# Last rows' weights ahead of the turning copies, a second turning tile, and two interleaved projections in a two-layer decoder trunk

## The chip, the cores and the metric

The kernel runs on one core of a Trainium2 chip. The metric is the time of one execution on the device, in microseconds, as the median of several runs. A profile of one execution goes with it. In profile rows PE is TensorE's matmuls, PEld its weight loads, DVE VectorE, ACT ScalarE, POOL GpSimd, SP SyncE; SPq and ACTq are DMA issues on SyncE's and ScalarE's queues.

## The reference

Two layers of a decoder for 256 tokens of width 2048, all in float32. Each layer is a mixer and a gated MLP, each with an RMS norm ahead and a residual sum behind:

```python
def reference(x, ...):
    for l in range(DEPTH):                  # 2
        h = rms_norm(x, mix_norm[l])
        h = mixer_ab(h, ...) if l % 2 == 0 else mixer_c(h, ...)
        x = x + h
        h = rms_norm(x, ffn_norm[l])
        x = x + conv_ffn(h, ffn_w_up[l], ffn_conv_w[l], ffn_conv_b[l], ffn_w_down[l])

def mixer_c(h, w_in, b_f, q_gain, k_gain, w_out):   # layer 1: attention with a forget gate
    q, k, v, g, f = jnp.split(h @ w_in, [D, 2*D, 3*D, 4*D], axis=-1)   # 16 heads of 128
    q, k = rms_norm(q, q_gain), rms_norm(k, k_gain)
    c = cumsum(log_sigmoid(f + b_f))                # one number a head and token
    s = q k^T * scale + c_query - c_key             # causal softmax in blocks of 128 queries
    return (softmax(s) @ v * sigmoid(g)) @ w_out

def conv_ffn(h, w_up, conv_w, conv_b, w_down):
    z = h @ w_up                                    # 2 x 5632 columns
    z = causal convolution of width 3 over tokens + conv_b
    a, b = jnp.split(z, 2, axis=-1)
    return (jax.nn.silu(a) * b) @ w_down
```

Mixer A/B of layer 0 (spatial gating and a gated linear recurrence) is not touched by the change.

## The kernel before

The residual stream x lies on chip as 16 blocks of 128 features by 256 tokens, in seven tiles (blocks 12 to 15 are one, x_76 in the program; blocks 8 to 11 are x_75). A norm (`Norm`) turns block m into a pair of tiles for TensorE, a high part rounded for the fast matmul and the rest: `feed_split`, L398 on ScalarE and L401 on VectorE. Weights are treated alike: each load of 512 KB on SyncE's queue (L198) gives a tile w, ScalarE copies its rounded part into wh (L185), VectorE subtracts the rest into wl (L186). Each product then takes three matmuls: high by high, high by rest, rest by high. Rings of five tiles for w and three for wh and wl, with some more in a second pool, let the loads run ahead.

A projection goes through k, the feature blocks, in pairs, one weight load a pair, and has the tokens' two halves T in two PSUM tiles. `project_tok` (L323) does it for four heads of q, k or v (L341 to L343 are its matmuls, 12 a pair), `project_four` (L346) for the MLPs and the output projections (L360 to L362), and `project` (L301) for one output block of 128 features with the features on partitions (L316).

A result with tokens on partitions has to be turned before it goes into x or into the heads. `blocks` turns 32 by 32 blocks on VectorE into a tile tmp (L373), and `moves` sends 16 small copies (L380) that put the blocks in their places, in turn on SyncE's queue and GpSimd's, for one quarter of the last MLP also on ScalarE's. `transposed` does both.

What runs beside the projections is written as generators: each call of `tick`, one ahead of every weight load, moves the waiting ones on by a step, so that their instructions land between the splits of the weights. `held` binds an instruction's place behind the last wh or wl before it. The framework's scheduler then sets each engine's order by its own estimates; no engine's queue is reordered on the chip.

Attention (`mixer_c`, from L941) begins with the first four heads' q and k, called `early` (L963 to L965): first all eight pairs of q, then all eight of k; `fetch` loads the forget gate's weights w_cf between. After them `drain` finishes the norm. `turn_rows` (L1137) then scales each of the two (L1140), squares and sums them for their norm (L433, L434, L1148) and turns them into `turn` tiles, which `attend` (L1041) takes. `forget` and `sums` (L976, L988) make c, a scan on VectorE (L1020), and send it through memory into cb (L1022, L1028).

In the MLP (`ffn`, L1254) `four` and `up` do the up-projection with the convolution, `down` the down-projection in four quarters q of four output blocks, summed over several groups of hidden features in y. In the last group `add_y` turns a quarter of y and adds it to x (L1335). In the last MLP the fourth quarter is done as four rows, blocks 12 to 15, by `project` (L1364); their result needs no turning and is added at L1368, and `finish_x` writes x out (L1351, L1353). There `room` gives one tile tmp and two tiles zt for the turning.

Of the kernel before, what the change touches and what calls it, by code (L numbers as in the profile page):

```python
# [55 lines left out]
def tile_trunk(ctx: ExitStack, tc: tile.TileContext, x, pp_d, cst_d, mlev_d, msk_d,  # L56
# [263 lines left out]
            done += c  # L320
        return ps

    def project_tok(wsrc, norm, room=None):  # L323

        ps = [pm.tile([P, 512], F32, tag="pm", name=nm("pm")) for _ in range(2)]
        for k in range(0, KT, 2):
            tick()
            wh, wl = weights(wsrc[:, k * 512:(k + 2) * 512], 1024, None, apart)
            if room is not None:
                ar = room()  # L330
                for i in range(2):
                    nc.gpsimd.tensor_copy(ar[:, i * S:(i + 1) * S].rearrange("p (u n) -> p u n", u=2),
                                          view(norm.a[k + i], S - 1, (S, 2), (-1, P)))
            for T in range(2):
                for i in range(2):
                    a = norm.a[k + i]
                    ah, al = a[:, T * P:(T + 1) * P], a[:, S + T * P:S + (T + 1) * P]
                    if T and room is not None:
                        ah, al = ar[:, i * S:i * S + P], ar[:, i * S + P:(i + 1) * S]
                    h, l = (by_two(t, i) for t in (wh, wl))  # L340
                    PE.matmul(to_two(ps[T]), ah, h, start=k + i == 0, stop=False)  # L341
                    PE.matmul(to_two(ps[T]), ah, l, start=False, stop=False)  # L342
                    deep["last"] = PE.matmul(to_two(ps[T]), al, h, start=False, stop=k + i == KT - 1)  # L343
# [597 lines left out]
    def mixer_c(norm):  # L941
# [18 lines left out]
            held(V.tensor_tensor(w2, w.rearrange("p (k c) -> p k c", k=KT)[..., 0:CH],  # L960
                                 pp[:, norm.col:norm.col + KT].unsqueeze(2).to_broadcast([P, KT, CH]), ALU.mult), "wl")

        early = [project_tok(w_cqkv[0], norm)]  # L963
        flight.append(fetch())
        early.append(project_tok(w_cqkv[CH // 4], norm))  # L965
        drain()
        depth[0] = 2
        Rt = norm.Rt
# [285 lines left out]
    def ffn(l, norm, last):  # L1254
# [5 lines left out]
        nxt = None if last else Norm(C_MIX + KT)  # L1260

        def room():
            return (hp.tile([P, 1024], F32, tag="tmp", name=nm("tmp"), bufs=1),
                    hp.tile([P, 4, S], F32, tag="zt", name=nm("zt"), bufs=2))

        def four(j0):
# [54 lines left out]

        y = hp.tile([P, 2, D], F32, tag="y", name=nm("y"))

        def add_y(q, finish):
            tmp, zt = room()
            near = last and q == 2
            transposed(lambda T: y[:, T, q * 512:(q + 1) * 512], tmp, zt,
                       (nc.sync, nc.gpsimd, SC) if near else (nc.sync, nc.gpsimd))

            def rest():  # L1330
                for _ in range(3 if near else LAG - 2 * (q == 3)):
                    yield
                for i in range(4):
                    m = 4 * q + i
                    held(V.tensor_tensor(xT[m], xT[m], zt[:, i], ALU.add), "wl")  # L1335
                    if finish:
                        finish_x(m)
                    if not near and (q < 3 or i % 2):
# [17 lines left out]

        def down(k0, hid, first, final):
            n = len(hid)
            for q in range(4):
                if last and final and q == 3:  # L1360
                    parts = None
                    for m in range(4 * q, KT):
                        end = m == KT - 1
                        ps = project(w_dn[l, m], hid, chunks=(n,), k0=k0, parts=parts)  # L1364
                        if not end:
                            tick()
                            parts = weights(w_dn[l, m + 1][:, k0 * P:(k0 + n) * P], n * P)
                        V.tensor_tensor(xT[m], xT[m], ps[:, 0:S], ALU.add)  # L1368
                        finish_x(m)
                    return  # L1370
                ps = project_four(w_dn[l, 4 * q:4 * q + 4], hid, n, k0)
                for T in range(2):
                    d = y[:, T, q * 512:(q + 1) * 512]
                    if first:
# [1 line left out]
                    else:  # L1376
                        V.tensor_tensor(cols4(d), cols4(d), of_rows(ps[T]), ALU.add)
                if final:
                    add_y(q, True)

        j0, k0, hid = 0, 0, []
        for g, (now, ahead) in enumerate(STEPS):
# [100 lines left out]
```

## Time and profile before

| | us |
|---|---|
| median of 3 runs (2170.22 to 2171.02) | 2170.75 |
| the profiled execution | 2170.68 |
| its span, first to last instruction | 2168.9 |
| TensorE busy with matmuls, 10874 of them | 2162.4 |
| VectorE busy | 1599.7 |
| ScalarE busy | 1310.1 |
| GpSimd busy | 470.7 |

The granted clock of TensorE is 1.0 over the span. HBM gives 202 GB/s on average. An instruction's row in order of time has its start, its duration, the engine and line, what it writes and reads, how many are merged, and, in brackets, how long its engine was idle before it and what released it.

### The profile page before, as it was taken

The page shows a single profiled execution, that of the slowest core. Times are in us where ns is not written, and L with a number is a line of the kernel's source. Part 1 is how long each engine was busy: PE and PEld are TensorE (multiplying, and loading weights), DVE is VectorE, ACT ScalarE, POOL GpSimd, SP SyncE. Part 2 cuts the span into 40 slices and gives each one's busy share as a digit, 9 for nine tenths or more (in the row PEclk, how much of TensorE's full clock was granted, in tenths as well). Part 3 has the DMA queues.
Part 4 walks back from the last instruction along what each step waited for, and adds up shares of the span by engine and source line. Part 5 has one row for each costly group of instructions (what it writes and reads, how often), then busy time and mean ns, then how long its engine had stood idle before and what let it go on. Part 6 is the DMA issues. An engine that isn't in the chain of part 4 may idle for free.

```text
span 2168.9 us, 32423 instructions
## 1 busy us (share of the span) xinstructions
PE 2162.4 (100%) x10874; PEld 1900.3 (88%) x10874; DVE 1599.7 (74%) x2265; ACT 1310.1 (60%) x1903; POOL 470.7 (22%) x867
## 2 busy tenths in 40 slices
PE   9999999999999999999999999999999999999999
PEld 8998888888888888888888888888888888888888
DVE  7888768777577657776887787877786577667766
ACT  6677766666466545654565556766666466456642
POOL 0352231212012002111133443221211012012102
PEclk9999999999999999999999999999999999999999
DMA  8755777777667767776777767777777677666866
GB/s 304 220 172 175 219 223 236 235 229 238 217 214 223 223 213 212 230 235 205 248 230 223 243 203 215 225 240 223 234 238 223 201 236 220 227 213 208 247 214 187
DMA packets 492680, 483.61 MB, mean 223 GB/s; under 512 B 115168, under 2 KB 460400, under 8 KB 492384
## 3 DMA queue, kind: packets, MB, share of 16 engines
q1 hardware_dynamic: 465888, 453.27, 66.4%
q0 software_dynamic: 24896, 26.05, 5.2%
q10 hardware_dynamic: 1728, 2.21, 0.4%
q8 instruction: 85, 1.39, 0.3%
q14 instruction: 83, 0.68, 0.1%
HBM read 435.24 MB, written 2.11 MB: 202 GB/s over the span
## 4 chain that ended last, share of the span: by engine, by line
PE 94%; DVE 2%; DMA 2%; SPq 1%; ACT 1%; issue 0%; DVEq 0%; ACTq 0%; POOLq 0%
PE pm L360 25%; PE pm L361 25%; PE pm L362 25%; PE pm L341 4%; PE pm L343 4%; PE pm L342 4%; PE pm L316 2%; PE pm L236 1%; DVE wl L186 1%; SPq L380 1%; DMA w<-in_w_up 1%; DMA zt<-tmp 1%; PE pm L260 0%; DVE tmp L373 0%; ACT wh L185 0%
## 5 line engine op out<-in xcount | busy, mean ns | idle before, releaser
L186 DVE TENSOR_TENSOR wl<-w,wh 128x1024 fp32r<-128x1024 f32 (+1 forms) x820 | 991.6, 1217 | 460.6 <-ACT wh L185 451.1
L185 ACT ACTIVATE wh<-w 128x1024 fp32r<-128x1024 f32 (+1 forms) x820 | 856.7, 1049 | 624.4 <-PE pm L362 459.3
L360 PE MATMUL pm<-wh,a 128*128 128x512 f32 x1728 | 655.8, 379 | 0.0
L361 PE MATMUL pm<-wl,a 128*128 128x512 f32 x1728 | 655.2, 379 | 0.2
L362 PE MATMUL pm<-wh,a 128*128 128x512 f32 x1728 | 654.9, 379 | 0.0
L380 POOL DMA_DIRECT2D zt<-tmp x413 | 223.5, 549 | 1134.8 <-DVE tmp L373 1022.9
L361 PEld LDWEIGHTS pm<-wl,a 128*128 128x128 f32 x1728 | 326.6, 189 | 47.1 <-DVE wl L186 1.0
L362 PEld LDWEIGHTS pm<-wh,a 128*128 128x128 f32 x1728 | 326.6, 189 | 46.3
L360 PEld LDWEIGHTS pm<-wh,a 128*128 128x128 f32 x1728 | 326.6, 189 | 46.3
L360 PE MATMUL pm<-wh,hid 128*128 128x512 f32 x688 | 260.8, 379 | 0.0
L361 PE MATMUL pm<-wl,hid 128*128 128x512 f32 x688 | 260.8, 379 | 0.0
L362 PE MATMUL pm<-wh,hid 128*128 128x512 f32 x688 | 260.8, 379 | 0.0
L341 PE MATMUL pm<-wh,a 128*128 128x512 f32 x416 | 158.7, 381 | 0.4 <-ACT a L398 0.4
L343 PE MATMUL pm<-wh,a 128*128 128x512 f32 x416 | 157.8, 379 | 0.0
L342 PE MATMUL pm<-wl,a 128*128 128x512 f32 x416 | 157.7, 379 | 0.0
L360 PEld LDWEIGHTS pm<-wh,hid 128*128 128x128 f32 x688 | 130.0, 189 | 18.5
L362 PEld LDWEIGHTS pm<-wh,hid 128*128 128x128 f32 x688 | 130.0, 189 | 18.4
L361 PEld LDWEIGHTS pm<-wl,hid 128*128 128x128 f32 x688 | 130.0, 189 | 18.4
L1289 ACT ACTIVATE conv<-zt,pp 128x256 f32<-128x256 f32 x176 | 95.8, 589 | 71.5 <-DMA zt<-tmp 48.4
L380 POOL DMA_DIRECT2D turn<-tmp x160 | 86.9, 551 | 211.4 <-DVE tmp L373 179.3
L1290 DVE SCALAR_TENSOR_TENSOR conv<-zt,pp,conv 128x255 f32<-128x255 f32 x176 | 80.2, 480 | 54.4 <-ACT conv L1289 42.7
L373 DVE STREAM_TRANSPOSE tmp<-z 128x512 f32<-128x512 f32 x120 | 98.1, 850 | 7.1 <-ACT z L1275 5.1
(255 smaller groups left out, 2207.7 us busy)
## 6 DMA issues: line engine op xcount, KB each, us to landing
w<-in_w_up SPq DMA_DIRECT2D x352, 512.0 KB, 5.0
w<-in_w_dn SPq DMA_DIRECT2D x176, 512.0 KB, 5.0
w<-in_w_cqkv SPq DMA_DIRECT2D x96, 512.0 KB, 4.9
w<-in_w_abo SPq DMA_DIRECT2D x32, 512.0 KB, 5.0
w<-in_w_cg SPq DMA_DIRECT2D x32, 512.0 KB, 5.2
w<-in_w_co SPq DMA_DIRECT2D x32, 512.0 KB, 4.8
zt<-tmp SPq DMA_DIRECT2D x414, 32.0 KB, 2.7
zt<-tmp POOLq DMA_DIRECT2D x413, 32.0 KB, 2.4
```

The lines of the kernel that those rows point to most:

```text
L185: r = deep["wh"] = SC.activation(wh, w, AF.Copy)
L186: deep["wl"] = V.tensor_tensor(wl, w, wh.bitcast(F32), ALU.subtract)
L341: PE.matmul(to_two(ps[T]), ah, h, start=k + i == 0, stop=False)
L342: PE.matmul(to_two(ps[T]), ah, l, start=False, stop=False)
L343: deep["last"] = PE.matmul(to_two(ps[T]), al, h, start=False, stop=k + i == KT - 1)
L360: PE.matmul(to_rows(ps[T]), ah, h, start=not begun and k + i == ks[0], stop=False)
L361: PE.matmul(to_rows(ps[T]), ah, l, start=False, stop=False)
L362: deep["mm"] = deep["last"] = PE.matmul(to_rows(ps[T]), al, h, start=False, stop=not more and k + i == ks[-1] + 1)
L373: V.transpose(tmp.rearrange("p (b m i t) -> p b m i t", b=4, m=4, t=2)[:, :, :, :, T], src(T).rearrange("p (m b j) -> p b m j", m=4, b=4))
L380: queues[(a + b) % len(queues)].dma_start(dst[BLK * b:BLK * (b + 1), :, a * n:(a + 1) * n], tmp[BLK * a:BLK * (a + 1), b * 4 * n:(b + 1) * ...
L1289: held(SC.activation(c, z, AF.Identity, bias=pp[:, cb:cb + 1], scale=w(2)))
L1290: V.scalar_tensor_tensor(c[:, 1:], z[:, :S - 1], w(1), c[:, 1:], ALU.mult, ALU.add)
```

## The change

It has three parts.

In the last MLP the weights of the last four rows are fetched and split in `split_rows`: two ahead of the sum of the third quarter into y, two more between that quarter's `blocks` and its `moves`, so all four ahead of the copies. Before, the first load stood at the row's `project` and each further one after the row ahead of it. `add_y` is split in two for it, the rows' loop has one `tick` more ahead, and the adds of the last two rows are bound behind the last add of the third quarter (`deep["near"]`).

In both MLPs `room` has two tiles tmp in place of one.

In the attention the q and k projections of the first four heads are cut in two: six pairs of q, six of k, then the last two pairs (blocks 12 to 15) of q, and of k.

```diff
--- before.py
+++ after.py
@@ -320,10 +320,10 @@
             done += c
         return ps
 
-    def project_tok(wsrc, norm, room=None):
-
-        ps = [pm.tile([P, 512], F32, tag="pm", name=nm("pm")) for _ in range(2)]
-        for k in range(0, KT, 2):
+    def project_tok(wsrc, norm, room=None, ks=range(0, KT, 2), ps=None):
+
+        ps = ps or [pm.tile([P, 512], F32, tag="pm", name=nm("pm")) for _ in range(2)]
+        for k in ks:
             tick()
             wh, wl = weights(wsrc[:, k * 512:(k + 2) * 512], 1024, None, apart)
             if room is not None:
@@ -960,9 +960,14 @@
             held(V.tensor_tensor(w2, w.rearrange("p (k c) -> p k c", k=KT)[..., 0:CH],
                                  pp[:, norm.col:norm.col + KT].unsqueeze(2).to_broadcast([P, KT, CH]), ALU.mult), "wl")
 
-        early = [project_tok(w_cqkv[0], norm)]
-        flight.append(fetch())
-        early.append(project_tok(w_cqkv[CH // 4], norm))
+        firsts = [w_cqkv[0], w_cqkv[CH // 4]]
+        early = []
+        for src in firsts:
+            early.append(project_tok(src, norm, ks=range(0, KT - 4, 2)))
+            if src is firsts[0]:
+                flight.append(fetch())
+        for src, ps in zip(firsts, early):
+            project_tok(src, norm, ks=range(KT - 4, KT, 2), ps=ps)
         drain()
         depth[0] = 2
         Rt = norm.Rt
@@ -1260,7 +1265,7 @@
         nxt = None if last else Norm(C_MIX + KT)
 
         def room():
-            return (hp.tile([P, 1024], F32, tag="tmp", name=nm("tmp"), bufs=1),
+            return (hp.tile([P, 1024], F32, tag="tmp", name=nm("tmp"), bufs=2),
                     hp.tile([P, 4, S], F32, tag="zt", name=nm("zt"), bufs=2))
 
         def four(j0):
@@ -1321,18 +1326,21 @@
 
         y = hp.tile([P, 2, D], F32, tag="y", name=nm("y"))
 
-        def add_y(q, finish):
+        def add_y(q, finish, between=None):
             tmp, zt = room()
             near = last and q == 2
-            transposed(lambda T: y[:, T, q * 512:(q + 1) * 512], tmp, zt,
-                       (nc.sync, nc.gpsimd, SC) if near else (nc.sync, nc.gpsimd))
+            blocks(lambda T: y[:, T, q * 512:(q + 1) * 512], tmp)
+            if between is not None:
+                between()
+            moves(tmp, zt, (nc.sync, nc.gpsimd, SC) if near else (nc.sync, nc.gpsimd))
 
             def rest():
                 for _ in range(3 if near else LAG - 2 * (q == 3)):
                     yield
                 for i in range(4):
                     m = 4 * q + i
-                    held(V.tensor_tensor(xT[m], xT[m], zt[:, i], ALU.add), "wl")
+                    deep["near"] = V.tensor_tensor(xT[m], xT[m], zt[:, i], ALU.add)
+                    held(deep["near"], "wl")
                     if finish:
                         finish_x(m)
                     if not near and (q < 3 or i % 2):
@@ -1356,19 +1364,26 @@
 
         def down(k0, hid, first, final):
             n = len(hid)
+            rows = []
+
+            def split_rows(count):
+                for m in range(KT - 4 + len(rows), KT - 4 + len(rows) + count):
+                    rows.append(weights(w_dn[l, m][:, k0 * P:(k0 + n) * P], n * P))
+
             for q in range(4):
                 if last and final and q == 3:
-                    parts = None
+                    tick()
                     for m in range(4 * q, KT):
-                        end = m == KT - 1
-                        ps = project(w_dn[l, m], hid, chunks=(n,), k0=k0, parts=parts)
-                        if not end:
+                        ps = project(w_dn[l, m], hid, chunks=(n,), k0=k0, parts=rows.pop(0))
+                        if m < KT - 1:
                             tick()
-                            parts = weights(w_dn[l, m + 1][:, k0 * P:(k0 + n) * P], n * P)
-                        V.tensor_tensor(xT[m], xT[m], ps[:, 0:S], ALU.add)
+                        r = V.tensor_tensor(xT[m], xT[m], ps[:, 0:S], ALU.add)
+                        if m >= KT - 2:
+                            tc.add_manual_dep(r.ins, deep["near"].ins.name, order, reason="not before")
                         finish_x(m)
                     return
                 ps = project_four(w_dn[l, 4 * q:4 * q + 4], hid, n, k0)
+                split_rows(2 if last and final and q == 2 else 0)
                 for T in range(2):
                     d = y[:, T, q * 512:(q + 1) * 512]
                     if first:
@@ -1376,7 +1391,7 @@
                     else:
                         V.tensor_tensor(cols4(d), cols4(d), of_rows(ps[T]), ALU.add)
                 if final:
-                    add_y(q, True)
+                    add_y(q, True, (lambda: split_rows(2)) if last and q == 2 else None)
 
         j0, k0, hid = 0, 0, []
         for g, (now, ahead) in enumerate(STEPS):
```

The matmuls and their number stay, and each engine's order changes in two places only, the beginning of the attention and the end of the program. SyncE at the beginning of the attention, before (w are weights; turn_10619 is q, turn_10624 is k, of the first four heads):

```order
L198 DMA w_10825<-in_w_cqkv 128x1024
L198 DMA w_10850<-in_w_cqkv 128x1024
L380 DMA turn_10619<-tmp_10621 32x4x64 x8
L198 DMA w_10876<-in_w_cqkv 128x1024
L198 DMA w_10908<-in_w_cqkv 128x1024
L380 DMA turn_10624<-tmp_10626 32x4x64 x8
L198 DMA w_10926<-in_w_cqkv 128x1024
```

and now:

```order
L198 DMA w_10825<-in_w_cqkv 128x1024
L198 DMA w_10850<-in_w_cqkv 128x1024
L198 DMA w_10876<-in_w_cqkv 128x1024
L380 DMA turn_10619<-tmp_10621 32x4x64 x8
L380 DMA turn_10624<-tmp_10626 32x4x64 x8
L198 DMA w_10908<-in_w_cqkv 128x1024
L198 DMA w_10926<-in_w_cqkv 128x1024
```

Both loads between the two groups of copies have left: one stands ahead of the first group, the other (w_10908, the first weights of the next heads' q) behind the second.

VectorE there, before, from the scaling of q (z_10620) to the turning of k (z_10625):

```order
L1148 TENSOR_TENSOR z_10620<-z_10620,ss_10618 128x512 x2
L186 TENSOR_TENSOR wl_10701<-w_10699,wh_10700 128x2x2x256
L373 STREAM_TRANSPOSE tmp_10621<-z_10620 128x512 x2
L186 TENSOR_TENSOR wl_10755<-w_10753,wh_10754 128x2x2x256
L433 TENSOR_TENSOR tmp_10626<-z_10625 128x512
L434 TENSOR_REDUCE ss_10618<-tmp_10626 128x4
L433 TENSOR_TENSOR tmp_10626<-z_10625 128x512
L434 TENSOR_REDUCE ss_10618<-tmp_10626 128x4
L186 TENSOR_TENSOR wl_10773<-w_10771,wh_10772 128x2x2x256
L425 TENSOR_SCALAR rm_10689<-ss_10618 128x2x4
L428 SCALAR_TENSOR_TENSOR rt_10690<-ss_10618 128x2x4
L429 TENSOR_TENSOR rt_10690<-rt_10690,rm_10689 128x2x4
```

and now:

```order
L434 TENSOR_REDUCE ss_10618<-tmp_10626 128x4
L1153 TENSOR_TENSOR z_10620<-z_10620,ss_10618 128x512 x2
L425 TENSOR_SCALAR rm_10689<-ss_10618 128x2x4
L373 STREAM_TRANSPOSE tmp_10621<-z_10620 128x512
L428 SCALAR_TENSOR_TENSOR rt_10690<-ss_10618 128x2x4
L373 STREAM_TRANSPOSE tmp_10621<-z_10620 128x512
L429 TENSOR_TENSOR rt_10690<-rt_10690,rm_10689 128x2x4
L186 TENSOR_TENSOR wl_10773<-w_10771,wh_10772 128x2x2x256
L430 SCALAR_TENSOR_TENSOR ss_10618<-rt_10690,ss_10618 128x2x4
L186 TENSOR_TENSOR wl_10791<-w_10789,wh_10790 128x2x2x256
L1153 TENSOR_TENSOR z_10625<-z_10625,ss_10618 128x512 x2
L373 STREAM_TRANSPOSE tmp_10626<-z_10625 128x512 x2
```

The turning of q has moved down behind the sums of squares of k, and two splits of weights stand ahead of the scaling of k where one stood.

A little before, ScalarE splits the last blocks of x for the norm. Before (a_10338 is block 10, a_10345 and a_10352 are blocks 12 and 13, a_10377 is block 11):

```order
L398 ACTIVATE a_10338<-x_75,pp 128x256
L455 ACTIVATE sq_10341<-x_75 128x256
L185 ACTIVATE wh_10416<-w_10415 128x2x2x256
L398 ACTIVATE a_10345<-x_76,pp 128x256
L455 ACTIVATE sq_10348<-x_76 128x256
L398 ACTIVATE a_10352<-x_76,pp 128x256
L455 ACTIVATE sq_10355<-x_76 128x256
L398 ACTIVATE a_10377<-x_75,pp 128x256
L455 ACTIVATE sq_10380<-x_75 128x256
```

and now:

```order
L398 ACTIVATE a_10338<-x_75,pp 128x256
L455 ACTIVATE sq_10341<-x_75 128x256
L185 ACTIVATE wh_10418<-w_10417 128x2x2x256
L398 ACTIVATE a_10345<-x_76,pp 128x256
L455 ACTIVATE sq_10348<-x_76 128x256
L398 ACTIVATE a_10352<-x_76,pp 128x256
L455 ACTIVATE sq_10355<-x_76 128x256
L398 ACTIVATE a_10377<-x_75,pp 128x256
L455 ACTIVATE sq_10380<-x_75 128x256
```

Nothing has moved there but the weight's number: block 11 stands behind blocks 12 and 13.

SyncE at the end, before (zt_20618 is the third quarter's turning, w_20745 the last row's weights, out<-x_76 the rows' results):

```order
L380 DMA zt_20518<-tmp_20517 32x4x64 x8
L1353 DMA out<-x_70 128x256
L1353 DMA out<-x_71 128x256
L1353 DMA out<-x_72 128x512
L198 DMA w_20745<-in_w_dn 128x1024
L380 DMA zt_20618<-tmp_20617 32x4x64 x6
L1351 DMA out<-x_76 128x256 x2
```

and now (zt_20630 and w_20639 are these):

```order
L380 DMA zt_20518<-tmp_20517 32x4x64 x8
L1361 DMA out<-x_70 128x256
L1361 DMA out<-x_71 128x256
L198 DMA w_20639<-in_w_dn 128x1024
L1359 DMA out<-x_76 128x256
L380 DMA zt_20630<-tmp_20629 32x4x64 x6
L1361 DMA out<-x_72 128x512
L1359 DMA out<-x_76 128x256
```

The last row's weights stand ahead of the write of x_72, and the first row's result is written ahead of the turning copies.

ScalarE at the end, before:

```order
L185 ACTIVATE wh_20640<-w_20639 128x1024
L185 ACTIVATE wh_20672<-w_20671 128x1024
L185 ACTIVATE wh_20706<-w_20705 128x1024
L380 DMA zt_20618<-tmp_20617 32x4x64 x5
L185 ACTIVATE wh_20746<-w_20745 128x1024
```

and now:

```order
L185 ACTIVATE wh_20616<-w_20615 128x1024
L185 ACTIVATE wh_20622<-w_20621 128x1024
L185 ACTIVATE wh_20634<-w_20633 128x1024
L185 ACTIVATE wh_20640<-w_20639 128x1024
L380 DMA zt_20630<-tmp_20629 32x4x64 x5
```

The split of the last row's weights has moved ahead of the five copies.

## The prediction

> **What bounds the kernel now.** I read the busy times first, then TensorE's waits, then the instructions by time at the two places that the change touches.
>
> ```profile
> span 2168.9 us, 32423 instructions
> PE 2162.4 (100%) x10874; PEld 1900.3 (88%) x10874; DVE 1599.7 (74%) x2265; ACT 1310.1 (60%) x1903; POOL 470.7 (22%) x867
> ```
>
> TensorE is busy for 2162.4 of 2168.9 us. The change leaves it the same matmuls, so nothing can be won beyond 6.5 us of idle time and the small gaps that the modelled ends hide. Of TensorE's waits the longest after the program's start is this one (total, times, longest):
>
> ```profile
> PE pm L341 <- ACT a L398: 0.4, 1, 0.4
> ```
>
> It lies in the attention layer's first projection; none lies in an MLP before the last rows. In order of time (start, duration, idle before), with the ScalarE split that releases it:
>
> ```profile
> 1057.06 0.49 ACT L398 ACTIVATE a<-x,pp 128x256 fp32r<-128x256 f32 x1
> 1057.60 0.48 PE L341 MATMUL pm<-wh,a 128*128 128x512 f32 x1 [0.42 <-ACT a L398]
> ```
>
> The rest of the idle time is the end. There, by engine (the four queues are TensorE, ScalarE's DMA issues and work, SyncE's issues, VectorE):
>
> ```profile
> 2161.48 0.61 PE L316 MATMUL pm<-hid,wh 128*128 128x256 f32 x4
> 2162.23 0.49 PE L316 MATMUL pm<-hid,wl 128*128 128x256 f32 x2
> 2163.90 0.61 PE L316 MATMUL pm<-hid,wh 128*128 128x256 f32 x4
> 2164.34 0.39 PE L316 MATMUL pm<-hid,wl 128*128 128x256 f32 x2
> ...
> 2155.56 4.17 ACTq L380 DMA_DIRECT2D zt<-tmp  x5
> 2159.86 1.06 ACT L185 ACTIVATE wh<-w 128x1024 fp32r<-128x1024 f32 x1 [10.34 <-DMA zt<-tmp]
> ...
> 2151.24 3.05 SPq L1353 DMA_DIRECT2D out<-x  x3
> 2154.34 0.42 SPq L198 DMA_DIRECT2D w<-in_w_dn  x1
> 2155.55 4.62 SPq L380 DMA_DIRECT2D zt<-tmp  x6
> 2164.64 1.21 SPq L1351 DMA_DIRECT2D out<-x  x2
> ...
> 2156.32 0.42 DVE L1368 TENSOR_TENSOR x<-x,pm 128x256 f32<-128x256 f32 x1 [0.53 <-PE pm L316]
> 2162.09 2.10 DVE L1335 TENSOR_TENSOR x<-x,zt 128x256 f32<-128x256 f32 x6
> 2164.77 0.42 DVE L1368 TENSOR_TENSOR x<-x,pm 128x256 f32<-128x256 f32 x1 [0.25 <-PE pm L316]
> ```
>
> The last row's weights are split only after ScalarE has issued five turning copies, so TensorE's wl matmuls begin 0.75 us after the wh matmuls ahead of them, where the last group needs 0.44 (2163.90 to 2164.34): 0.3 us lost, and 0.1 more in the longer wl matmuls (0.49 against 0.39). VectorE's last add ends at 2165.19, and SyncE's last write-out and its landing end the span at 2168.9.
>
> **The last rows' weights: +1.0 us.** The 0.4 us on TensorE goes away. What matters is what is late next. In the new order SyncE loads the last row's weights right after the two small writes (2152.33, where the third write of x stood, against 2154.34), and ScalarE splits them before its five copies instead of behind them. The landing times of the weight loads in this stretch (least, median, most):
>
> ```profile
> DMA to landing us min/median/max: 3.9/4.6/5.9
> ...
> zt<-tmp ACTq DMA_DIRECT2D x5, 32.0 KB, 3.1
> ```
>
> I take 3.9, since no other weight load stands behind this one: landed at 2156.2, split until 2157.3, so ScalarE's copies begin at 2157.4 instead of 2155.56, 1.8 us later. On SyncE the six copies now stand behind the write of row 12, which waits for its add (2156.32 + 0.42): 2156.8, then 0.5 for the issue, so 2157.3 instead of 2155.55. Both queues that carry the third quarter's turning are some 1.8 us late. In the old run ScalarE had issued its copies by 2155.56 + 4.17 = 2159.73, the last begun some 0.6 earlier, at 2159.1; now it begins at 2160.9 and lands 3.1 later (the second row above) at 2164.0. Four adds of 0.35 (2.10 / 6) bring 2165.4, and the new order keeps the adds of rows 14 and 15 behind them: 0.35 + 0.42, so 2166.2 against 2165.19. That is 1.0 us later, and the write-out follows as before. With 4.6 for the load it is 1.7, with 5.9 it is 3.0; if the copies catch up entirely, only the 0.4 us of TensorE is left as a gain. I keep +1.0, in -0.4 to +3.0.
>
> The Trainium skill (Trainium Kernel Development and Optimization, Key Constraints) says that issuing DMAs from several engines only saves the sequencers' issue time. By that rule the late start on ScalarE could be moved to any queue without loss, but the new order fills both queues at once; no run here separates the two.
>
> **The interleaved projections: +1.5 us.** First, what they do not remove. TensorE's stall at 1057.60 is for normed block 11 (sixth pair, second half). The new order still needs block 11 in its sixth pair, and ScalarE still splits 12 and 13 ahead of it. So the 0.4 us stays; only blocks 12 to 15 get more time, and nothing waits for them now. The load of w_cf goes ahead of one weight load; the splits there run some 5 us ahead of their use, which hides it.
>
> Second, what they delay. The first projection now ends two pairs (5.2 us) before the second instead of eight. Its squares, scaling and turning on VectorE fall together with those of the second, and its eight SyncE copies come directly before the second's eight, where a weight load or two stood between. The old run:
>
> ```profile
> 1085.33 5.12 SPq L380 DMA_DIRECT2D turn<-tmp  x8
> 1090.54 1.02 SPq L198 DMA_DIRECT2D w<-in_w_cqkv  x2
> 1094.33 5.10 SPq L380 DMA_DIRECT2D turn<-tmp  x8
> ...
> 1081.40 1.29 DVE L1148 TENSOR_TENSOR z<-z,ss 128x512 f32<-128x512 f32 x2
> 1086.29 0.67 DVE L433 TENSOR_TENSOR tmp<-z 128x512 f32<-128x512 f32 x1
> 1092.75 1.55 DVE L373 STREAM_TRANSPOSE tmp<-z 128x512 f32<-128x512 f32 x2
> 1103.41 1.19 DVE L186 TENSOR_TENSOR wl<-w,wh 128x1024 fp32r<-128x1024 f32 x1
> ...
> 1102.23 1.04 ACT L185 ACTIVATE wh<-w 128x1024 fp32r<-128x1024 f32 x1
> 1104.80 1.06 ACT L185 ACTIVATE wh<-w 128x1024 fp32r<-128x1024 f32 x1 [1.53 <-DMA w<-in_w_cqkv]
> 1105.77 0.45 ACT L1054 ACTIVATE k<-turn,gq 128x128 f32<-128x128 f32 x1
> 1108.03 1.04 ACT L185 ACTIVATE wh<-w 128x1024 fp32r<-128x1024 f32 x1
> 1109.10 0.69 ACT L1167 ACTIVATE vh<-pm,Rt 128x512 fp32r<-128x512 f32 x1
> ...
> 1109.47 0.38 PE L342 MATMUL pm<-wl,a 128*128 128x512 f32 x1
> 1114.65 0.38 PE L342 MATMUL pm<-wl,a 128*128 128x512 f32 x1
> ...
> DMA to landing us min/median/max: 3.6/4.8/6.3
> ```
>
> VectorE went from the second projection's first square (1086.29) to the end of its turning (1092.75 + 1.55 = 1094.3). Now the first projection's scaling (1.29) and turning (1.55), three small operations (0.6 together) and one more wl (1.2) lie between, and 0.7 of idle time and a small operation go: 1098.3. Only then does SyncE issue the second eight copies, 5.1 us, and behind them the weights of the next projection's first pair (the load that went out at 1090.54 + 0.6): 1103.5. They land 4.8 later (the median of this stretch; 3.6 and 6.3 are its ends) at 1108.3, wh takes 1.06, wl 1.2: 1110.6. TensorE read this wl at 1109.47, so it waits 1.15. Behind that, ScalarE's new order is wh, wh, the two copies of v (1.15 from 1109.10 on), the heads' splits (1105.77 to 1108.03, 2.3), and only then the third pair's wh: 1109.4 + 1.06 + 1.15 + 2.3 + 1.04 = 1114.9, its wl 1116.15, against 1114.65 + 1.15: another 0.35. Together 1.5; with 3.6 it is 0.3, with 6.3 it is 3.0.
>
> By the Trainium skill (DMA: Bandwidth & Descriptors, Anatomy of one DMA) a load takes about 2.0 us plus its bytes over 436 GB/s, an estimate of 3.2 us for 512 KB, with which this stall would be 0; the 4.8 us of the row speaks against it.
>
> **The second turning tile: 0.** Where VectorE waits at the turning line, it is
>
> ```profile
> DVE tmp L373 <- ACT z L1275: 5.1, 18, 0.8
> ```
>
> for ScalarE's z, and no row of VectorE's waits has it waiting there for the copies that read tmp. The order of all engines in the MLPs, up to the end, is unchanged, and TensorE waits for nothing there. Were the 5.1 us hidden waits for tmp after all, they would be 18 of 0.3 us, under TensorE's pairs of 2.6. I take 0, in -0.4 to 0.
>
> **Sum.** 1.0 + 1.5 + 0 = +2.5 us. The profiled execution took 2170.68 us, 1.8 more than its span, and the median is 2170.75: 2173.2 us.
>
> **Rivals.**
> Room enough (0.18): the loads land at their shortest, 3.6 and 3.9, and the turning copies overtake what they lost. Then 0.3 at the attention and 0 at the end: 2171.0. For it speaks that half the loads land below the median; against it, that the late copies at the end follow from an add and a split, not from a load.
> The stalls go (0.08): the 0.4 at the end, block 11's 0.4, as much again in the slowed matmuls behind it, and 0.4 hidden in the MLPs: 2170.75 - 1.6 = 2169.1. Against it: block 11's split keeps its place, and the end is set by adds.
> The forget gate becomes late (0.12), the case on the slower side of the bound below. Its scan stands behind the turning on VectorE, two copies through memory behind it, and the scores wait for these:
>
> ```profile
> 1102.81 0.68 DVE L1020 TENSOR_TENSOR_SCAN rows<-rows 16x256 f32<-16x256 f32 x1
> 1118.02 0.35 DVE L1073 SCALAR_TENSOR_TENSOR sc<-px,ct,cb 128x128 f32<-128x128 f32 x1 [1.07 <-PE px L1068]
> ...
> cb<-cd POOLq DMA_DIRECT2D x4, 512.0 KB, 4.2
> cd<-rows POOLq DMA_DIRECT2D x1, 16.0 KB, 4.9
> ```
>
> With the same delay of 4 us and its root moved behind the turning (0.9), the scan ends at 1108.4, and 4.9 + 4.2 later, 1117.5, the sums are there, 0.5 before their use. It decides from 0.5 us more. Three more put 2.5 us of waiting on VectorE at 1118 and, wl being queued behind it, on TensorE: 2173.2 + 2.5 = 2175.7. Against it: VectorE has idle time in that stretch that could take up the delay.
>
> **How the numbers follow.** The forecast has 0.62. Its own range runs from the smaller bounds (0.3 and 0.3: 2171.3) to one of the larger (3.0 + 1.0, or 1.5 + 3.0: 2175.2). With the rivals I reach from 2169.9 to 2176.0; outside lie most of the stalls' rival and the worst of the last. About 0.2% (4.3 us) is what a measurement can tell from no change, so 2166.4 and 2175.1 are the bounds: faster 0.01, since even all stalls together do not give it; slower 0.17 (the forget gate's case and 0.05 of the forecast); the same 0.82.
>
> **What would show it.** In the new profile TensorE should wait at L341/L342 near 1110 and 1116 us, for ACT or DVE, behind a weight load issued near 1103.5; the wait for block 11 near 1057.6 should still be there. At the end no idle time before the wl matmuls, the ScalarE copies starting after 2157, and VectorE's adds of rows 8 to 11 ending after row 15's matmuls. I am wrong if the next projection's first weights go out before 1102.3, or if the last add follows TensorE's end at once. TensorE's clock or matmul count changing would also break it.

## The result, and the profile after

The changed kernel takes 2174.49 us (median of 22 runs, 2173.57 to 2175.89), the kernel before in the same comparison 2170.8 (22 runs, 2169.28 to 2172.95): a ratio of 1.0018, with a 95% interval of 1.0012 to 1.0024, or 3.7 us more in median. The forecast was 2173.2 in 2169.9 to 2176.0, and "the same" within 0.2%. The time lies in the range. The interval does not contain 1, so the change does cost a little. The reason given for the time holds only in part.

The page of the changed kernel, and TensorE's waits over the whole span (total, times, longest):

```profile
span 2172.8 us, 32416 instructions
PE 2163.1 (100%) x10874; PEld 1902.9 (88%) x10874; DVE 1599.0 (74%) x2265; ACT 1310.0 (60%) x1903; POOL 470.5 (22%) x867
```

```profile
PE warm L143 <- DVE ones L85: 1.1, 1, 1.1
PE pm L342 <- DVE wl L186: 0.4, 2, 0.2
```

The span has grown by 3.9 us, TensorE's busy time by 0.7. The wait for block 11 (L341), before the longest behind the program's start, is gone, and two waits at L342, for the weights' rest, are new. They are the two that the prediction named. Small as they are, they can't make 3.9 us. The end can. The waits of the last 23 us:

```profile
POOL zt L380 <- DVE x L1342: 10.0, 1, 10.0
ACT wh L185 <- DMA w<-in_w_dn: 7.6, 1, 7.6
DVE x L1342 <- DMA out<-x: 4.3, 1, 4.3
```

and the same stretch in order of time, engine by engine (TensorE, VectorE, ScalarE, GpSimd, SyncE):

```profile
2164.51 0.39 PE L316 MATMUL pm<-hid,wl 128*128 128x256 f32 x2
...
2155.04 0.76 DVE L373 STREAM_TRANSPOSE tmp<-y 128x512 f32<-128x512 f32 x1
2156.89 0.42 DVE L1380 TENSOR_TENSOR x<-x,pm 128x256 f32<-128x256 f32 x1 [1.10 <-PE pm L316]
2158.73 1.23 DVE L186 TENSOR_TENSOR wl<-w,wh 128x1024 fp32r<-128x1024 f32 x1 [1.42 <-ACT wh L185]
2159.88 1.42 DVE L1342 TENSOR_TENSOR x<-x,zt 128x256 f32<-128x256 f32 x4
...
2166.63 1.43 DVE L1342 TENSOR_TENSOR x<-x,zt 128x256 f32<-128x256 f32 x4 [4.33 <-DMA out<-x]
2167.98 0.74 DVE L1380 TENSOR_TENSOR x<-x,pm 128x256 f32<-128x256 f32 x2
...
2157.64 1.06 ACT L185 ACTIVATE wh<-w 128x1024 fp32r<-128x1024 f32 x1 [7.55 <-DMA w<-in_w_dn]
2160.66 3.51 ACTq L380 DMA_DIRECT2D zt<-tmp  x5
...
2160.93 2.71 POOL L380 DMA_DIRECT2D zt<-tmp  x5 [10.02 <-DVE x L1342]
...
2152.92 1.26 SPq L198 DMA_DIRECT2D w<-in_w_dn  x1
2157.34 0.33 SPq L1359 DMA_DIRECT2D out<-x  x1
2160.66 3.82 SPq L380 DMA_DIRECT2D zt<-tmp  x6
```

Three queues start the third quarter's turning copies within 0.3 us of each other, at 2160.66, 2160.66 and 2160.93, although their own queues were free at different times: SyncE at 2157.34 + 0.33, ScalarE at 2157.64 + 1.06 = 2158.70 at the latest, and GpSimd had nothing to do for 10 us. What they read, tmp, was complete at 2155.04 + 0.76 = 2155.80. So they wait for something common that comes near 2160.6, and GpSimd's row names it: an add at L1342 on VectorE. In the group of four that starts at 2159.88 the first two adds end 0.76 later, at 2160.64. These are the adds of blocks 2 and 3, of the first quarter. They read the first quarter's zt tile. The MLP has two zt tiles, used in turn, so the third quarter's copies write into that very tile. The name in the row is a sign and not yet a proof: in the kernel before the same wait names an add as well,

```profile
POOL zt L380 <- DVE x L1335: 5.5, 1, 5.5
```

though there the copies on SyncE started at 2155.55 (in the prediction's rows), right behind the end of the turning at 2155.52, and no add of the shared tile was open. own_zt below is the test.

In the kernel before, the last of these adds stood ahead of two more splits of weights:

```profile
2147.65 0.43 DVE L1335 TENSOR_TENSOR x<-x,zt 128x256 f32<-128x256 f32 x1
```

It ended at 2148.08, 7.5 us before the copies wanted the tile. Now it ends at 2160.64, behind the last row's wl, since `held` keeps these adds in the written order of the splits and all four splits are written ahead of them. The last add of all ends at 2167.98 + 0.74 = 2168.72 instead of 2165.19; TensorE's last matmuls end at 2164.51 + 0.39 = 2164.90 instead of 2164.73. The 3.5 us between the two ends of the last add are nearly all of the loss. (The row of the 4.33 us names a write-out as the releaser. Those adds read zt; the last of SyncE's copies begins at 2163.9, and the last five copies of the three queues took 2.1 to 2.7 us from issue to landing, so I read the wait as the copies'. The profile of inter8 below, with the same end, names the copies for it: 4.27 us, zt<-tmp.)

The other place, the attention (SyncE, ScalarE, VectorE, TensorE of the changed kernel):

```profile
1091.41 11.43 SPq L380 DMA_DIRECT2D turn<-tmp  x16
1102.93 8.03 SPq L198 DMA_DIRECT2D w<-in_w_cqkv  x7
...
1107.06 1.06 ACT L185 ACTIVATE wh<-w 128x1024 fp32r<-128x1024 f32 x1 [2.54 <-DMA w<-in_w_cqkv]
1109.37 0.69 ACT L1172 ACTIVATE vh<-pm,Rt 128x512 fp32r<-128x512 f32 x1
...
1094.84 1.55 DVE L373 STREAM_TRANSPOSE tmp<-z 128x512 f32<-128x512 f32 x2
1104.99 0.68 DVE L1025 TENSOR_TENSOR_SCAN rows<-rows 16x256 f32<-16x256 f32 x1
1118.91 0.35 DVE L1078 SCALAR_TENSOR_TENSOR sc<-px,ct,cb 128x128 f32<-128x128 f32 x1 [0.52 <-PE px L1073]
...
1109.42 0.48 PE L342 MATMUL pm<-wl,a 128*128 128x512 f32 x1 [0.20 <-DVE wl L186]
1115.04 0.48 PE L342 MATMUL pm<-wl,a 128*128 128x512 f32 x1 [0.16 <-DVE wl L186]
```

Sixteen copies stand in one block on SyncE, the next weights go out at 1102.93 behind them and reach ScalarE 4.1 us later, and TensorE waits twice. A matmul of this shape follows the one before it after 0.216 us; counted against that pace the two waits, with the slower matmul behind each, cost 0.55 and 0.43, together 0.98 us. The first wait hangs on the landing: ScalarE, too, had waited 2.54 us for these weights. The second stands behind ScalarE's own work: from 1108.29 on it goes without a break through the second pair's wh, the two copies of v and the splits of the heads, and comes to the third pair's wh only at 1112.68.

The turning of k (L373) was complete at 1094.84 + 1.55 = 1096.39, 6.5 us before the weights went out. What SyncE was busy with until then is the sixteen copies themselves, 0.71 us each: those of k had to wait for those of q.

### The profile page after: what moved, and what is told of

Read it like the earlier page. It is cut to its first block, busy times and chain, and to the rows that moved or that the text cites. A ratio compares the mean times of both kernels' runs of the same rounds, so it can differ in the third digit from the quotient of the medians.

```text
span 2172.8 us, 32416 instructions
## 1 busy us (share of the span) xinstructions
PE 2163.1 (100%) x10874; PEld 1902.9 (88%) x10874; DVE 1599.0 (74%) x2265; ACT 1310.0 (60%) x1903; POOL 470.5 (22%) x867
## 4 chain that ended last, share of the span: by engine, by line
PE 95%; SPq 1%; DMA 1%; DVE 1%; ACT 1%; issue 0%; DVEq 0%; ACTq 0%
PE pm L360 26%; PE pm L361 26%; PE pm L362 26%; PE pm L341 4%; PE pm L342 4%; PE pm L343 4%; PE pm L316 2%; PE pm L236 1%; SPq L380 1%; DMA w<-in_w_dn 0%; ACT wh L185 0%; DMA w<-in_w_v 0%; DVE wl L186 0%; PE pm L260 0%; PE px L1073 0%
## 5 line engine op out<-in xcount | busy, mean ns | idle before, releaser
L341 PE MATMUL pm<-wh,a 128*128 128x512 f32 x416 | 158.8, 382 | 0.0
L342 PE MATMUL pm<-wl,a 128*128 128x512 f32 x416 | 158.0, 380 | 0.4 <-DVE wl L186 0.4
L373 DVE STREAM_TRANSPOSE tmp<-z 128x512 f32<-128x512 f32 x120 | 97.9, 850 | 7.2 <-ACT z L1280 5.3
```

The costliest lines, as they stand in the source:

```text
L373: V.transpose(tmp.rearrange("p (b m i t) -> p b m i t", b=4, m=4, t=2)[:, :, :, :, T], src(T).rearrange("p (m b j) -> p b m j", m=4, b=4))
```

## Experiments

Two theories stand against each other for the end. The **held buffer**: the copies wait for the adds of blocks 2 and 3, because they share a zt tile. The **late queues** (the prediction's): the weight load, the split and the write of row 12 stand ahead of the copies on their queues. In the table the gap is the end of the last add less the end of TensorE's last matmul, in the profiled execution; waits earlier in the span hardly enter it. Each ratio is against runs of the kernel before made beside it.

| kernel | median us | before | ratio (95%) | gap at the end, us |
|---|---|---|---|---|
| before | 2170.75 | | | 0.46 |
| the changed kernel | 2174.49 | 2170.80 | 1.0018 (1.0012 to 1.0024) | 3.82 |
| tail_only | 2174.26 | 2170.63 | 1.0017 (1.0008 to 1.0026) | 4.40 |
| own_zt | 2169.73 | 2170.63 | 0.9996 (0.9988 to 1.0005) | 0.46 |
| inter_only | 2170.90 | 2170.63 | 1.0001 (0.9992 to 1.0009) | |
| tmp2_only | 2170.13 | 2170.63 | 0.9998 (0.9990 to 1.0007) | |
| late_copies | 2170.82 | 2170.59 | 1.0000 (0.9991 to 1.0009) | 1.13 |
| adds_first | 2171.02 | 2170.59 | 1.0001 (0.9992 to 1.0011) | 0.89 |
| adds_first_plain | 2170.38 | 2170.59 | 1.0000 (0.9991 to 1.0009) | 0.46 |
| inter8 | 2173.50 | 2170.59 | 1.0017 (1.0008 to 1.0025) | |
| best_own | 2169.24 | 2170.22 | 0.9997 (0.9988 to 1.0005) | 0.46 |
| best_two | 2168.91 | 2170.22 | 0.9994 (0.9985 to 1.0003) | 0.46 |

An interval is about 1.9 us to each side. What is smaller is read from the profiles, or stays open.

### tail_only: the end alone

```diff
 (against the changed kernel)
-firsts = [w_cqkv[0], w_cqkv[CH // 4]]
...
+early = [project_tok(w_cqkv[0], norm)]
+flight.append(fetch())
+early.append(project_tok(w_cqkv[CH // 4], norm))
...
-tag="tmp", name=nm("tmp"), bufs=2
+tag="tmp", name=nm("tmp"), bufs=1
```

> The kernel before with the end alone changed (last four rows' weights early, order of the last adds); one turning tile, projections not interleaved. Held-buffer theory: the turning copies of the third quarter write into the zt tile that the first quarter's adds still read; those two adds (blocks 2 and 3) now stand behind the last row's wl, so both queues start their copies near 2160 us instead of 2155.55, the last adds end 3 to 3.5 us later than before, and the time is 2174 us (before + 3.2). Late-queues theory (the prediction's): the copies start at 2157.4, and the time is before + 1.0 = 2171.8.

Measured: 2174.26, 3.6 us over the kernel before. Its waits in the last 23 us, and VectorE and SyncE in order of time:

```profile
POOL zt L380 <- DVE x L1337: 10.6, 1, 10.6
```

```profile
2160.85 1.42 DVE L1337 TENSOR_TENSOR x<-x,zt 128x256 f32<-128x256 f32 x4
2168.97 0.74 DVE L1375 TENSOR_TENSOR x<-x,pm 128x256 f32<-128x256 f32 x2
2161.63 3.82 SPq L380 DMA_DIRECT2D zt<-tmp  x6
```

The end alone gives the whole loss, with the same picture: the copies start 0.78 us after the adds of the shared tile do. The second turning tile has no part in it.

### own_zt: the same, with a zt tile that nobody reads

```diff
 (against tail_only)
-def room():
+def room(tag="zt", n=2):
...
-            hp.tile([P, 4, S], F32, tag="zt", name=nm("zt"), bufs=2))
+            hp.tile([P, 4, S], F32, tag=tag, name=nm("zt"), bufs=n))
...
-tmp, zt = room()
 near = last and q == 2
+tmp, zt = room("zn", 1) if near else room()
```

> As tail_only, but the third quarter's turning has a zt tile of its own, so its copies need not wait for the first quarter's adds. Held-buffer theory: SyncE's copies start right after the turning on VectorE (near 2155.8 us), the adds of rows 8 to 11 end by 2165.5, and the time is 3 us under tail_only, 2170.5 to 2171.3. Late-queues theory: the weight load, the split and the write of row 12 still stand ahead of the copies, so they start at 2157.4 and the time is that of tail_only within 0.5 us.

Measured: 2169.73, 4.5 us under tail_only, and 0.8 under the least that was expected. VectorE, GpSimd and SyncE at the end:

```profile
2160.07 1.09 DVE L1337 TENSOR_TENSOR x<-x,zt 128x256 f32<-128x256 f32 x3
2161.41 2.43 DVE L1337 TENSOR_TENSOR x<-x,zt 128x256 f32<-128x256 f32 x7
2164.59 0.42 DVE L1375 TENSOR_TENSOR x<-x,pm 128x256 f32<-128x256 f32 x1 [0.42 <-PE pm L316]
...
2155.82 2.70 POOL L380 DMA_DIRECT2D zt<-tmp  x5 [5.28 <-DVE tmp L373]
...
2155.56 3.85 SPq L380 DMA_DIRECT2D zt<-tmp  x6
2160.85 0.34 SPq L1356 DMA_DIRECT2D out<-x  x1
```

The adds of blocks 2 and 3 stand where they stood, at 2160.07, but no copy waits for them: GpSimd is released by the turning itself (L373), SyncE starts at 2155.56, and the last add follows TensorE's end. This is what GpSimd's row alone could not show. The late-queues theory expected no difference. On SyncE the copies now also stand ahead of the writes of blocks 2 and 3 and of row 12, though only the tile was changed: their place behind row 12's write had come with the held tile, through the scheduler's estimates.

### late_copies: the order of tail_only, with the tile free

Since the order on SyncE changed in own_zt as well, this kernel keeps the own tile and binds the copies behind the write of row 12 on SyncE and behind the last row's wh on ScalarE, as in tail_only.

```diff
 (against own_zt)
+if eng in late:
+    tc.add_manual_dep(r.ins, late[eng].ins.name, order, reason="queue order")
...
-moves(tmp, zt, (nc.sync, nc.gpsimd, SC) if near else (nc.sync, nc.gpsimd))
+if near:
+    deep["moves"] = lambda r: moves(tmp, zt, (nc.sync, nc.gpsimd, SC), late={nc.sync: r, SC: deep["wh"]})
+else:
+    moves(tmp, zt)
...
+if m == 4 * q:
+    deep["moves"](deep["out"])
+    tick()
```

> As own_zt (the third quarter's zt tile its own, so nothing holds its copies), but the order on SyncE, ScalarE and VectorE is that of tail_only: SyncE's six copies behind the write of row 12, ScalarE's five behind the last row's split. This prices the prediction's mechanism alone. Late-queues theory: SyncE's copies start near 2157.5 us and ScalarE's near 2158.8; the last of ScalarE's begins near 2161.7 and lands 2 to 3 us later, six operations on VectorE follow, and the last add ends 1 to 1.9 us later than in own_zt: 2170.7 to 2171.6. If the order does not matter once the tile is free, own_zt's 2169.7 within 0.4.

Measured: 2170.82, 1.1 us over own_zt in median. VectorE, ScalarE and SyncE:

```profile
2163.27 1.43 DVE L1343 TENSOR_TENSOR x<-x,zt 128x256 f32<-128x256 f32 x4 [0.74 <-DMA zt<-tmp]
2164.62 0.75 DVE L1381 TENSOR_TENSOR x<-x,pm 128x256 f32<-128x256 f32 x2
...
2157.94 3.33 ACTq L381 DMA_DIRECT2D zt<-tmp  x5
...
2157.06 4.14 SPq L381 DMA_DIRECT2D zt<-tmp  x6
```

This is the picture that the prediction had drawn: copies from 2157.1 and 2157.9, VectorE waiting for them, rows 14 and 15 added last. The split of the last row's weights on ScalarE starts at 2157.86 and its copies at 2157.94: they do not wait for the end of the split, as the prediction had it. Its gap is 0.67 us above own_zt's. Of the 4.5 us between tail_only and own_zt, 3.4 are the held tile (2174.26 less 2170.82) and 1.1 the late queues. For the first the runs leave no doubt (2173.57 to 2175.52 against 2170.36 to 2172.29); the second is not clear by the times alone, but the gap agrees with it, if with less than the 1 to 1.9 expected. Against the kernel before, from which the prediction counted its +1.0, late_copies is 0.2 us slower in median, which is not told from none.

### adds_first: the tile read out in time

```diff
 (against the changed kernel)
-if not near and (q < 3 or i % 2):
+if not near and (q < 3 or i % 2) and not (last and q == 0 and i):
     yield
```

> The changed kernel whole, with one line more: in the last layer the first quarter's adds of blocks 1 to 3 run at once instead of one per step, so the shared zt tile is read out before the last row's wl comes up on VectorE. No extra tile. Held-buffer theory: the third quarter's copies start near 2155.8, the last add follows TensorE's end within 0.5 us, and the time is that of the changed kernel less 3.5 to 4.5: 2170.0 to 2171.0. Rival (the tile was only one of several holds): no more than 1.5 us is won, 2173 or more.

Measured: 2171.02, 3.5 us under the changed kernel in median, with a gap of 0.89 instead of at most 0.5. VectorE and SyncE of adds_first:

```profile
2160.35 1.22 DVE L186 TENSOR_TENSOR wl<-w,wh 128x1024 fp32r<-128x1024 f32 x1 [3.47 <-ACT wh L185]
2151.49 3.14 SPq L1361 DMA_DIRECT2D out<-x  x3
2154.68 0.42 SPq L198 DMA_DIRECT2D w<-in_w_dn  x1
```

One line frees the tile without spending memory. With blocks 2 and 3 done early, their write-out again stands ahead of the last row's weights, which go out at 2154.68; that makes wl late and leaves VectorE with seven adds behind it, the rest of the gap. adds_first_plain is the same without the interleaving:

```diff
 (against adds_first)
-firsts = [w_cqkv[0], w_cqkv[CH // 4]]
...
+early = [project_tok(w_cqkv[0], norm)]
+flight.append(fetch())
+early.append(project_tok(w_cqkv[CH // 4], norm))
```

> adds_first without the interleaved projections: last rows' weights early, second turning tile, early adds. If the interleaving costs 0.2 to 1.0 us, this is that much under adds_first: 2169.5 to 2170.2, and the best of all kernels here. If the interleaving is free, the two agree within 0.2.

It took 2170.38, 0.6 less, which the times can't tell from none. Its three writes, in the same place, took 2.42 us instead of 3.14, its last weights went out at 2153.22, and its gap is 0.46: the 0.89 is that of one execution. Both kernels lie at or 0.2 above the upper end of what was expected, and adds_first_plain is not the best of all: own_zt and the two last kernels below are lower in median.

### inter_only and inter8: the interleaved projections

inter_only has the two hunks of the change at `project_tok` and `early`, and nothing else of it.

> The kernel before with the interleaved projections alone. Late-weights theory: the next projection's first weights go out behind the second eight turning copies near 1103, TensorE waits for wl near 1109.5 and 1115 (together 1.0 us as in the changed kernel): before + 1.0 = 2171.8, or + 0.6 if the wait for block 11 near 1057.5 is also gone because of the interleaving. Rival: the two waits come from somewhere else in the change (the second tile): then no waits here, and the time of before.

Measured: 2170.90, 0.3 over the kernel before instead of the 0.6 to 1.0 expected. SyncE:

```profile
1091.08 10.86 SPq L380 DMA_DIRECT2D turn<-tmp  x16
1102.03 15.71 SPq L198 DMA_DIRECT2D w<-in_w_cqkv  x11
```

The same sixteen copies took 0.57 us less than in the changed kernel and began 0.33 earlier, the weights went out 0.9 earlier, and TensorE's two waits shrank to 0.08, as much as in the kernel before, and 0.22 against its pace (in adds_first, with this order too, the copies took 11.37 and the waits 0.37 and 0.43). The order makes the waits possible; how long they are, 0.3 to 1.0 us in three executions, goes with the time of the copies. Block 11's wait was there, 0.17 of idle time. inter8 changes one size:

```diff
 (against the changed kernel)
-early.append(project_tok(src, norm, ks=range(0, KT - 4, 2)))
+early.append(project_tok(src, norm, ks=range(0, KT - 8, 2)))
...
-project_tok(src, norm, ks=range(KT - 4, KT, 2), ps=ps)
+project_tok(src, norm, ks=range(KT - 8, KT, 2), ps=ps)
```

> The changed kernel with one size changed: the projections are interleaved from the fifth pair on, not from the seventh, so the first ends four pairs (10 us) ahead of the second, and one weight load goes out between the two groups of eight turning copies. Late-weights theory: the next projection's first weights go out about 0.5 us earlier or more, and TensorE's waits near 1109.5 and 1115 us (0.44 and 0.33 above the usual pace in the changed kernel) shrink to under 0.3 together. Rival (the waits belong to ScalarE's order behind the v copies): both stay. The time, set by the end, stays at 2173.5 to 2174.5.

SyncE in inter8:

```profile
1084.46 5.12 SPq L380 DMA_DIRECT2D turn<-tmp  x8
1089.68 1.01 SPq L198 DMA_DIRECT2D w<-in_w_cqkv  x2
1093.45 6.28 SPq L380 DMA_DIRECT2D turn<-tmp  x8
1099.83 16.52 SPq L198 DMA_DIRECT2D w<-in_w_cqkv  x10
```

The copies are in two groups again, two loads went out between them, the weights behind them follow 3 us earlier, and both waits at L342 are gone, as is the one for block 11, which is now needed four pairs later. The time, 2173.50, is still the end's. So the waits come with the position of the copies. That the order on ScalarE has no part in them is not shown: in inter8 it has changed too, the heads' splits and the third pair's wh stand ahead of the v copies there (1104.86, 1107.11 and 1108.17). For the first wait ScalarE's row in the changed kernel names the load; the second needs both, the late load and the work ahead of the third wh.

### tmp2_only: the second turning tile

```diff
 (against the kernel before)
-tag="tmp", name=nm("tmp"), bufs=1
+tag="tmp", name=nm("tmp"), bufs=2
```

> The kernel before with the second turning tile alone. If the second tile removed the waits at 880 us (0.3) and 1057.6 us (0.4) of the kernel before, both are absent here and the time is before - 0.7 = 2170.0. If they come and go between executions, or block 11's hangs on the interleaving, at least one is still here and the time is that of before within 0.4 us.

Measured: 2170.13, 0.5 under the kernel before, within what can't be told from none. Block 11's wait was there (0.18 of idle time). The one near 880 us, in the first MLP, which the profiles of the kernel before, tail_only, own_zt and best_own show, was absent, as in every kernel with two tiles here, but late_copies and inter_only have one tile and don't show it either. Whether the second tile does anything stays open; the 0.5 lies within the 1.9 that the times leave open.

### best_own and best_two: what the pieces give together

best_own is own_zt with inter8's order. best_two is adds_first with inter8's order and the third quarter's copies on two queues:

```diff
 (best_two against adds_first)
-range(0, KT - 4, 2) ... range(KT - 4, KT, 2)
+range(0, KT - 8, 2) ... range(KT - 8, KT, 2)
...
-moves(tmp, zt, (nc.sync, nc.gpsimd, SC) if near else (nc.sync, nc.gpsimd))
+moves(tmp, zt, (nc.sync, nc.gpsimd))
```

> own_zt (end: last rows' weights early, third quarter's zt tile its own, one turning tile) with the projections interleaved from the fifth pair on, as in inter8. If inter8's profile holds (no wait for block 11 near 1057 us, none near 1109 and 1115) and the end is own_zt's, TensorE's chain reaches to its last matmul, and the time is own_zt less 0.4: 2169.2 to 2169.7, the best of all. If inter8's missing waits were one execution's chance, own_zt's time.

> adds_first with the interleaving of inter8, and the third quarter's copies on SyncE and GpSimd alone, so that ScalarE is free to split the last row's weights as soon as they land. If the copies on ScalarE cost adds_first its last 0.4 to 0.9 us, this gives 2169.3 to 2170.3; if eight copies on SyncE land too late for the adds, 2170.5 to 2171.5.

Measured: 2169.24, as expected, and 2168.91, 0.4 under what was expected. ScalarE and SyncE of best_two:

```profile
2157.72 1.06 ACT L185 ACTIVATE wh<-w 128x1024 fp32r<-128x1024 f32 x1 [9.27 <-DMA w<-in_w_dn]
2154.34 5.16 SPq L380 DMA_DIRECT2D zt<-tmp  x8
```

Eight copies on SyncE instead of six are issued by 2159.50, and the gap at the end is 0.46, as in adds_first_plain, where three queues carried them: ScalarE's queue was not needed. The Trainium skill (Trainium Kernel Development and Optimization, Key Constraints) says that several issuing engines save issue time only; this run agrees: the issues on SyncE take 5.16 us instead of the 3.98 of adds_first_plain, and the end is the same. best_two is 5.6 us under the changed kernel and 1.3 under the kernel before. The first is clear, the second is not (0.9985 to 1.0003).

## Why the prediction was right or wrong

**The verdict and the time** were right: the same within 0.2%, on the slow side, 2173.2 against 2174.49. The +2.5 us came out as +3.7, and that sum is near in part by luck: the end was put 2.6 us too low (against tail_only's +3.6), the attention, by the profile, about 0.5 too high, and block 11's 0.4 went away, which was forecast to stay.

**The last rows' weights** were mis-sized, +1.0 in -0.4 to +3.0 against +3.6 in tail_only, outside the bounds. The step that failed is the start of the copies, "ScalarE's copies begin at 2157.4 ... so 2157.3 instead of 2155.55" on SyncE. They began at 2160.66 on both. The mechanism named there exists: late_copies, which has it alone, shows copies from 2157.1 and 2157.9. It is smaller than forecast: its last add ends 1.13 us behind TensorE's end, where the sum has 1.9 (2166.2 against 2164.73 less the 0.4 that TensorE gains), and against the kernel before it costs 0.2 in median. Two errors in it nearly cancel on ScalarE: the load took 5.4 us there (4.6 in the changed kernel) and not the least time of 3.9, but the copies did not wait for the end of the split. What was missing is a reader. The prediction asked of each queue what stands ahead of the copies, and never who still reads the tile that they write. A sign of it stood in the rows of SyncE's order ahead of the prediction: the write of x_72 had moved behind the copies, so its adds had most likely moved too, and these adds read zt. The expected landmarks at the end came out all the same (no idle time of TensorE, copies after 2157, the adds of rows 8 to 11 behind the last matmul), and so did not tell the two causes apart; the 10 us of GpSimd's wait pointed to the right one, on the one queue of the three that the prediction had not looked at, and own_zt showed it.

**The interleaved projections**: +1.5 in 0.3 to 3.0 against 0.98 in the changed kernel's profile, and 0.3 to 1.0 over three executions. The landmarks came out: weights out at 1102.93 (1103.5 predicted, with 1102.3 as the bound), waits at 1109.42 and 1115.04 (near 1110 and 1116), the second behind ScalarE's order as described. One step of the path to them is wrong: the prediction let the second eight copies begin at 1098.3, when VectorE has turned k, and take 5.1. The turning was over at 1096.39; the copies of k stood behind those of q, which began at 1091.41, and the sixteen took 11.43 together. That both ways end near 1103 is luck. The sizes were not right either: the weights went out 0.6 earlier and landed in 4.1 us (1102.93 to 1107.06) instead of 4.8, so wl was ready 1.2 sooner than forecast; but TensorE, too, was 0.4 us ahead of the kernel before (at 1070 us), the earlier waits being gone, and the first wait came out at 0.55 instead of 1.15. The Trainium skill (DMA: Bandwidth & Descriptors, Anatomy of one DMA) gives the 2.0 us plus bytes over 436 GB/s for GpSimd's path, and this load goes by SyncE's queue; as an estimate for it the page's figures make 3.2 us, and the row's 4.1 stands between that and the 4.8.

**"Block 11's 0.4 us stays"** was wrong for this execution and right for its order: the order kept it (0.17 us in inter_only), but its size goes with the landing of copies, below.

**The second tile**: 0 in -0.4 to 0; -0.5 in tmp2_only's median, not told apart from none.

**The rivals.** Room enough fell: both places lost time. The stalls go: two of them went (block 11's, in this execution, and the end's 0.4), under a larger loss. The forget gate: its scan ended at 1105.67, not 1108.4, and the scores waited 0.52 for TensorE, against 1.07 before, not for the sums; it was not late.

## What to carry to other kernels

When work is moved ahead on an engine, list what now stands behind it and which buffers that work still reads: with a ring of two tiles one small add can hold all writers two rounds later, on all queues at once. Several queues that start at the same instant, after different idle times, are a sign of one common reader or writer; look for it in the row of the queue that waited longest, and test it with a buffer of its own. Measure the end of a program as the distance from the bounding engine's last instruction to the last one of all, so that waits earlier in the span do not blur it.

## What was not expected of the hardware

The same turning copies, at the same place of the same order, land later in one execution than in another. These are the eight on SyncE between 1043 and 1060 us, 32 KB each, in the profiles of the kernels that need block 11 in the sixth pair:

| kernel | the eight issues, us | issue to landing, median | latest | TensorE idle before block 11 |
|---|---|---|---|---|
| before | 5.92 | 3.6 | 4.2 | 0.42 |
| tail_only | 6.50 | 3.0 | 4.2 | 0.37 |
| tmp2_only | 6.30 | 2.2 | 3.9 | 0.18 |
| inter_only | 6.18 | 2.2 | 3.8 | 0.17 |
| own_zt | 6.11 | 2.2 | 3.7 | not listed |
| adds_first_plain | 5.97 | 2.5 | 3.7 | not listed |
| adds_first | 5.88 | 2.2 | 3.7 | not listed |
| late_copies | 6.02 | 2.2 | 3.6 | not listed |
| the changed kernel | 5.76 | 2.2 | 3.4 | not listed |

TensorE's wait for block 11 stands behind these copies, by way of VectorE's adds and ScalarE's split, and it goes with the latest landing, not with the median: there is none up to 3.7 us. tail_only and own_zt differ in the last MLP alone, far behind this place, so the edit is not what sets the landing. So a wait of a few tenths behind a DMA, seen in one profile, is no fixed cost of the kernel. Why the landings differ was not found; no run tried it.
